# Attention of the second network: two heads at a time on halves of the array, and one VectorE pass for bias and maximum

## The chip, the cores and the metric

The kernel runs on one core of a Trainium2 chip. The metric is the device time of one execution in microseconds (us), as the median of several. The core has a matrix engine (TensorE, in the profile PE for the products and PEld for the loads of the stationary operand), VectorE (DVE), ScalarE (ACT), GpSimd (POOL) and SyncE (SP), which here issues most DMA transfers. The engines run side by side, each through its own list of instructions, and wait for one another by semaphores.

## The reference

Two networks are computed, one behind the other, each of attention mixers and feed-forward blocks on 256 context rows and 256 latent rows of width 1024. The change touches the two mixers of the second network. The first, called Mla here, has 8 heads with queries and keys of 128 "nope" and 64 "rope" columns; the rope part of the keys is shared by all heads. Latent rows see all 512 keys, context rows the 256 context keys:

```python
def _mla_kv(h, w_dkv, kv_norm, w_ukv, rows, cols):
    ckv = h @ w_dkv
    c_kv, k_pe = ckv[..., :MLA_KV_RANK], ckv[..., MLA_KV_RANK:]
    kv = (_rms_norm(c_kv, kv_norm) @ w_ukv).reshape(b, s, MLA_HEADS, MLA_NOPE + MLA_V)
    ...
def _mla_mixer(h, hc, w_dq, q_norm, w_uq, w_dkv, kv_norm, w_ukv, w_o, need_ctx):
    scale = (MLA_NOPE + MLA_ROPE) ** -0.5
    q = _mla_q(h, w_dq, q_norm, w_uq, rows, cols)
    k_all = jnp.concatenate([kc, k], 1)
    v_all = jnp.concatenate([vc, v], 1)
    out = _block_attention(q[:, :, :, None], k_all, v_all, scale) @ w_o
    if need_ctx:
        out_c = _block_attention(qc[:, :, :, None], kc, vc, scale) @ w_o
```

The second, called Na, has 16 heads of 64 columns. Latent rows see the 256 context keys and, with a bias and a mask, the 256 latent keys:

```python
s_lat = jnp.einsum('bqhd,bkhd->bhqk', q_row, k_strip).astype(jnp.float32) * scale + bias
s_lat = jnp.where(mask, s_lat, -jnp.inf)
s_ctx = jnp.einsum('bqhd,bkhd->bhqk', q_row, kc).astype(jnp.float32) * scale
p = jax.nn.softmax(jnp.concatenate([s_ctx, s_lat], -1), axis=-1).astype(v.dtype)
return jnp.einsum('bhqk,bkhd->bqhd', p, jnp.concatenate([vc, v_strip], 1))
```

## The kernel before

Activations are held transposed, with features on the 128 partitions. The projections around the attentions (L291 to L293) run three passes per tile, since each operand is split into a high and a low part; weights come by SyncE's DMA into `wraw`, and ScalarE (L221) and VectorE or GpSimd (L229) split them. Products land in eight PSUM banks that `bank()` hands out in turn, and `tt()` hands out the temporaries for exponentials and their transposes.

An attention is cut into units of one head and one block of 128 query rows. Mla has 32 units, 8 heads with row blocks `qt` in the order 2, 0, 3, 1, of which 2 and 3 have 512 keys and 0 and 1 have 256. Na has 32 units, 16 heads with two row blocks, all of 512 keys; two heads share a tile `t`, one on partitions 0 to 63 and one on 64 to 127 of queries and keys.

`attention()` walks through the units in steps and writes the order by hand: within `in_order`, TensorE, VectorE and ScalarE get their instructions in just the order in which the code issues them. In one step stand, for units of different age:

- the scores of the newest unit (`at_scores`, lag 0): Na L2318, on the 64 partitions of its head; Mla L2119 on all 128 partitions (nope) and L2123 on 64 (rope). Operands are fp32, and each such matmul is two passes.
- the turn of the unit of three steps ago (`at_turn`): transposes of the weights on TensorE L1972, 128 keys each, and a copy to `wT` on ScalarE L1974
- VectorE's part, woven instruction by instruction from three lists: the softmax of the newest unit (Na only: bias addition L2327, in PSUM on the 256 latent keys; then maximum L1953, its scaling L1954, with the exponential on ScalarE L1956), the normalization of the unit of two steps ago (reciprocal L1960, scaling L1961), and `lo`, the low part L1999 of a finished tile
- `hi`, the high part of a finished tile, copied by ScalarE L1992
- the value products of the unit of four steps ago (`at_out`): Mla L2147 on 128 columns, Na L2347 on the 64 columns of its head, which is `tile_position=(0, 64 * q)`. The tile of output is finished, and handed to `hi` of the next step, every four units in Na and in Mla.

Na's biases are chunks of 512 KB for two heads, in `wraw`; one is freed and one asked for every four steps. The last three steps (33 to 35) hold pieces of the output projection (`MLA_FILL`, `NA_FILL`), and Na's steps 28 to 31 split some of its weights on ScalarE and GpSimd. `low_apply` (rms norm and gain of Mla's queries and latent keys), `k_post` (Na's keys with their bias) and `prep` run ahead of the attentions.

Of the kernel before, what the change touches and what calls it, by code (L numbers as in the profile page):

```python
# [92 lines left out]
def build(nc, tc, ctx, A, stop=None):  # L93
# [1856 lines left out]
    def softmax(ps, nk, scale):  # L1950

        mx, rs = small(1), small(1)
        yield V.reduce_max(mx, ps[:, 0:nk], axis=AX.X)  # L1953
        yield V.tensor_scalar(mx, mx, -scale, None, ALU.mult)  # L1954
        e = tt()[:, 0:nk]
        ACT.activation(out=e, in_=ps[:, 0:nk], func=AF.Exp, scale=scale, bias=mx, accum_out=rs)  # L1956
        return e, rs
# [23 lines left out]
    def attention(units, mixer, before=lambda step: None, after=lambda step: None):  # L1981

        done, half = [], []

        def out(u):
            got = mixer.at_out(u)
            if got:
                done.append(got)
# [12 lines left out]
        def steps():  # L2001
            for step in range(len(units) + 4):
                before(step)
                at = {lag: units[step - lag] for lag in range(5) if 0 <= step - lag < len(units)}
                for lag, f in ((0, mixer.at_scores), (3, mixer.at_turn)):
                    if lag in at:
                        do(f, at[lag])
                do(lambda at=at: weave(*[f(at[lag]) for lag, f in ((0, mixer.at_soft), (2, mixer.at_norm)) if lag in at], lo()))
                do(hi)
                if 4 in at:  # L2010
                    do(out, at[4])
                after(step)
            do(hi)
            do(lambda: weave(lo()))
# [29 lines left out]
    class Mla:  # L2044
# [32 lines left out]
        def low_apply(self, name, nk, g):  # L2077
            M = self.M
            bc = rms_spread(M[name + "r"], FULL)
            M[name + "h"] = R[name] = h = HL(nk)  # L2080
            for k in range(nk):
                t = tt()[:, 0:512]
                V.scalar_tensor_tensor(t, M[name][:, k * 512:(k + 1) * 512], v(g, k), bc, ALU.mult, ALU.mult)
                split_act(t, h.at(0, k, FULL), h.at(1, k, FULL))
# [26 lines left out]
        def at_scores(self, u):  # L2111
            M = self.M
            hd, qt = u
            if "am" not in M:
                M["am"] = R["am"] = HL(8)
            nk = 256 if qt < 2 else 512
            ps = bank()
            o = hd % 4 * 512
            PE.matmul(ps[:, 0:nk], M["qn", hd // 4][:, o + qt * 128:o + qt * 128 + 128], M["kn", hd // 4][:, o:o + nk], start=True,  # L2119
                      stop=False)  # L2120
            p = slice(64 * (hd % 2), 64 * (hd % 2) + 64)
            o = hd // 2 * 512 + qt * 128
            PE.matmul(ps[:, 0:nk], M["qp", 0][p, o:o + 128], M["ckv"][p, 1024:1024 + nk], start=False, stop=True)  # L2123
            M["s", u] = ps

        def at_soft(self, u):
            M = self.M
            M["e", u] = yield from softmax(M.pop(("s", u)), 256 if u[1] < 2 else 512, (128 + 64) ** -0.5)
# [8 lines left out]
        def at_out(self, u):  # L2137
            M = self.M
            hd, qt = u
            nk = 256 if qt < 2 else 512  # L2140
            if qt == 2:
                M["po"] = bank()
            po = M["po"]
            wT = M.pop(("w", u))
            for j in range(nk // 128):
                vo = (j % 2) * 1024 + hd * 128
                PE.matmul(po[:, qt * 128:(qt + 1) * 128], M["v", j // 2][:, vo:vo + 128], wT[:, j * 128:(j + 1) * 128],  # L2147
                          start=j == 0, stop=j == nk // 128 - 1)
            if qt == 1:
                return po, hd, FULL  # L2150

        def middle(self):
# [42 lines left out]
            attention([(hd, qt) for hd in range(8) for qt in (2, 0, 3, 1)], self, early)  # L2195
# [63 lines left out]
    class Na:  # L2259
# [15 lines left out]
        def k_post(self, t, seg, ps):  # L2275
# [4 lines left out]
            ACT.activation(out=N["k", t // 4][:, o + seg.start:o + seg.stop], in_=ps, func=AF.Identity, bias=v("b_qk", 8 + t))  # L2280
# [29 lines left out]
        def at_scores(self, u):  # L2310
            N = self.N
            hd, qt = u
            if "am" not in N:
                N["am"] = R["am"] = HL(8)
            t, q = divmod(hd, 2)
            p = slice(64 * q, 64 * q + 64)
            ps = bank()
            PE.matmul(ps, N["q"][p, t * 256 + qt * 128:t * 256 + qt * 128 + 128], N["k", t // 4][p, (t % 4) * 512:(t % 4 + 1) * 512],  # L2318
                      start=True, stop=True)
            N["s", u] = ps  # L2320

        def at_soft(self, u):
# [4 lines left out]
            yield V.tensor_tensor(ps[:, 256:512], ps[:, 256:512], raw[:, bo:bo + 256], ALU.add)  # L2327
            N["e", u] = yield from softmax(ps, 512, 1.0)
# [8 lines left out]
        def at_out(self, u):  # L2337
            N = self.N
            hd, qt = u
            t, q = divmod(hd, 2)  # L2340
            if q == 0 and qt == 0:
                N["po"] = bank()
            po = N["po"]
            wT = N.pop(("w", u))
# [4 lines left out]
            if q == 1 and qt == 1:  # L2349
                return po[:, 0:256], t, X  # L2350

        def middle(self):
# [7 lines left out]
            units = [(hd, qt) for hd in range(16) for qt in range(2)]  # L2360
# [224 lines left out]
```

## Time and profile before

| | us |
|---|---|
| median of 3 runs (2868.4 to 2869.3) | 2868.72 |
| the profiled execution | 2867.64 |
| its span in the trace | 2865.9 |
| TensorE busy, products | 2780.0 (97%) |
| VectorE busy | 2012.6 (70%) |
| ScalarE busy | 1117.9 (39%) |
| GpSimd busy | 240.6 (8%) |

Busy time is counted over the whole span and says nothing of a single stage. The attention steps of Mla lie between 1902 and 1993 us after the span's start, those of Na between 2526 and 2621. A row of a timeline has the start in us, the duration, the engine, the line, the operation, what it writes and reads, the shapes of both (of a TensorE row first the rows and columns of the array that it uses), the number of instructions that stand in one row, and in brackets how long the engine idled before it, and for whom. A row of a table of windows has the stretch, its length, then each engine's busy time and number of instructions in the order PE, PEld, DVE, ACT, POOL, then the mean granted clock, the DMA share and GB/s. Recorded ends overlap the next start on the same engine a little, so the cost of a thing in a row of work is read from start to start.

### The profile page before, as it was taken

Reading aid. Unit: us, or ns where it says so; the run is one execution under the profiler, and the core shown is the slowest. Engines: PE = TensorE matmul, PEld = TensorE weight load, DVE = VectorE, ACT = ScalarE, POOL = GpSimd, SP = SyncE. Lnnn points to the kernel's source line nnn. Section 1 sums busy time; section 2 is a strip of 40 time slices with the busy share of each in tenths; the row PEclk is TensorE's granted clock in tenths of the full one; section 3 lists DMA queues with packets and bytes.
Section 4 is the critical chain, followed back from the end, with each engine's and each line's share of the span. In section 5 each row is a group of like instructions: output and inputs, shape, how many; then the busy total and the mean of one; then the engine's idle time right before and its main releaser. Section 6 shows DMA issues by size and latency. Waiting matters only on the chain. (4 is left out here: it accounts for less than half of the span.)

```text
span 2865.9 us, 41032 instructions
## 1 busy us (share of the span) xinstructions
PE 2780.0 (97%) x15940; PEld 2383.6 (83%) x15940; DVE 2012.6 (70%) x3847; ACT 1117.9 (39%) x1947; POOL 240.6 (8%) x184
## 2 busy tenths in 40 slices
PE   7999999999999999999999999999999999998998
PEld 4888888878888888888889999866888888966898
DVE  5877776567877788787845755734888848357766
ACT  3222235654222232222355544444522334335544
POOL 0000011221000010000210100100300003003200
PEclk9999999999999999999999999999999999999999
DMA  6655632112665636665532465320166631413453
GB/s 262 203 198 189 200 117 91 52 45 82 206 201 188 200 118 209 207 206 176 174 118 82 138 200 178 96 67 15 60 213 207 195 97 59 143 42 102 141 183 105
DMA packets 114068, 413.15 MB, mean 144 GB/s; under 512 B 12496, under 2 KB 14800, under 8 KB 112336
## 3 DMA queue, kind: packets, MB, share of 16 engines
q1 hardware_dynamic: 112256, 407.64, 44.0%
q10 hardware_dynamic: 1616, 2.88, 0.3%
q8 instruction: 125, 2.05, 0.3%
q14 instruction: 71, 0.58, 0.1%
HBM read 409.42 MB, written 1.05 MB: 143 GB/s over the span
## 5 line engine op out<-in xcount | busy, mean ns | idle before, releaser
L292 PE MATMUL p<-slot,whl 128*128 128x512 f32 (+2 forms) x4256 | 1444.3, 340 | 16.2 <-DVE slot L652 6.2
L291 PE MATMUL p<-slot,whl 128*128 128x512 f32 (+2 forms) x4256 | 1445.5, 342 | 6.3 <-ACT slot L589 2.9
L293 PE MATMUL p<-slot,whl 128*128 128x512 f32 (+2 forms) x4256 | 1440.6, 339 | 6.6 <-DVE whl L229 5.0
L292 PEld LDWEIGHTS p<-slot,whl 128*128 128x128 f32 x4256 | 811.1, 191 | 111.0 <-POOL slot L753 8.0
L291 PEld LDWEIGHTS p<-slot,whl 128*128 128x128 f32 x4256 | 807.7, 191 | 106.0 <-issue 8.2
L293 PEld LDWEIGHTS p<-slot,whl 128*128 128x128 f32 x4256 | 810.5, 191 | 94.9 <-DVE whl L229 6.5
L221 ACT ACTIVATE whl<-wraw 128x1024 fp32r<-128x1024 f32 (+1 forms) x527 | 542.8, 1043 | 510.5 <-PE p L293 292.0
L229 DVE TENSOR_TENSOR whl<-wraw,whl 128x1024 fp32r<-128x1024 f32 (+1 forms) x460 | 561.1, 1222 | 196.3 <-ACT whl L221 188.5
L396 DVE SCALAR_TENSOR_TENSOR t<-wraw,sB 128x1024 bf16<-128x1024 f32 x448 | 535.0, 1219 | 3.0 <-ACT sB L150 3.0
L229 POOL TENSOR_TENSOR whl<-wraw,whl 128x1024 fp32r<-128x1024 f32 (+1 forms) x67 | 166.8, 2497 | 2085.3 <-ACT whl L221 2059.8
L1069 ACT ACTIVATE t<-p 128x512 f32<-128x512 f32 (+1 forms) x86 | 47.2, 548 | 536.2 <-PE p L293 536.2
L1071 DVE TENSOR_TENSOR t<-t,p 128x512 f32<-128x512 f32 (+1 forms) x86 | 53.8, 626 | 215.0 <-PE p L293 158.0
L291 PE MATMUL p<-whl,slot 128*128 128x256 f32 (+1 forms) x432 | 126.2, 292 | 0.0
L292 PE MATMUL p<-whl,slot 128*128 128x256 f32 (+1 forms) x432 | 124.3, 288 | 1.8 <-DVE whl L229 1.8
L293 PE MATMUL p<-whl,slot 128*128 128x256 f32 (+1 forms) x432 | 124.0, 287 | 0.0
L811 DVE SCALAR_TENSOR_TENSOR xT<-p,mod,xT 128x256 f32<-128x256 f32 x192 | 86.0, 478 | 33.0 <-PE p L293 32.7
L590 DVE TENSOR_TENSOR slot<-t,slot 128x512 fp32r<-128x512 f32 (+1 forms) x166 | 101.5, 617 | 3.3 <-ACT slot L589 2.9
L589 ACT ACTIVATE slot<-t 128x512 fp32r<-128x512 f32 (+1 forms) x166 | 89.2, 541 | 19.1 <-DVE t L2228 7.6
L824 DVE SCALAR_TENSOR_TENSOR xT<-p,mod,xT 128x256 f32<-128x256 f32 x119 | 54.4, 479 | 50.5 <-PE p L293 50.1
L556 DVE TENSOR_TENSOR t<-t 128x256 f32<-128x256 f32 (+1 forms) x98 | 74.7, 762 | 19.6 <-ACT t L555 18.4
L291 PEld LDWEIGHTS p<-whl,slot 128*128 128x128 f32 x432 | 82.9, 192 | 4.0 <-issue 2.3
L292 PEld LDWEIGHTS p<-whl,slot 128*128 128x128 f32 x432 | 83.0, 192 | 3.4 <-DVE whl L229 2.2
(309 smaller groups left out, 2047.5 us busy)
## 6 DMA issues: line engine op xcount, KB each, us to landing
wraw<-in_ada SPq DMA_DIRECT2D x224, 512.0 KB, 4.1
wraw<-in_ffn_in SPq DMA_DIRECT2D x176, 512.0 KB, 4.4
wraw<-in_mlp SPq DMA_DIRECT2D x128, 512.0 KB, 3.6
wraw<-in_ffn_out SPq DMA_DIRECT2D x64, 512.0 KB, 4.4
wraw<-in_ffn_out SPq DMA_DIRECT2D x32, 384.0 KB, 3.8
slot<-in_ada SPq DMA_DIRECT2D x8, 1024.0 KB, 16.2
wraw<-in_even_a SPq DMA_DIRECT2D x16, 512.0 KB, 3.4
wraw<-in_odd_a SPq DMA_DIRECT2D x16, 512.0 KB, 3.6
```

What stands on the lines that cost most here:

```text
L221: ACT.activation(out=hl[:, 0, 0:n], in_=raw[:, 0:n], func=AF.Copy)
L229: eng.tensor_tensor(hl[:, 1, 0:n], raw[:, 0:n], f32(hl[:, 0, 0:n]), ALU.subtract)
L291: PE.matmul(ps, w[0], a[0], start=first, stop=False)
L292: PE.matmul(ps, w[0], a[1], start=False, stop=False)
L293: R["pe"] = PE.matmul(ps, w[1], a[0], start=False, stop=last).ins
L396: V.scalar_tensor_tensor(j.bitcast(BF16)[:, 0:1024], raw, 1.0, sB[:, r, :], ALU.mult, ALU.mult, accum_out=mods[li][:, f, r:r + 1])
L556: V.tensor_tensor(a, a, sq[:, seg], ALU.add)
L589: ACT.activation(out=hi, in_=src, func=AF.Copy)
L590: (eng or V).tensor_tensor(lo, src, f32(hi), ALU.subtract)
L811: V.scalar_tensor_tensor(xT[:, m, SEGS[s]], ps[:, q - seg.start:q - seg.start + 256], mod(li, gate)[:, m, s:s + 1], xT[:, m, SEGS[s]], ALU ...
L824: V.scalar_tensor_tensor(xT[:, m, SEGS[s]], ps[:, q - seg.start:q - seg.start + 256], mod(li, gate)[:, m, s:s + 1], xT[:, m, SEGS[s]], ALU ...
L1071: V.tensor_tensor(sa[:, 0:w], sa[:, 0:w], pb, ALU.mult)
```

## The change

Units are taken by two heads of the same row block. Scores are issued for two heads at once, on odd steps, for the two steps to come (the first two before step 0), and behind the turn. In Mla the nope products of both heads stand first, then the rope products, which use the two row halves; in Na the two heads' products use the two row halves. Value products are issued for two heads at once on odd steps; in Na they alternate between the two column halves.

Mla's score scale goes into the gain of the query norm, and its maximum is written negated, so that the scaling of the maximum falls away. Na's context keys are stored negated, and its exponential has scale −1; a minimum over the context keys (L2343 of the changed kernel) and one fused pass over the latent keys (L2344), which forms −(score + bias), writes it and takes the minimum along, take the place of bias addition, maximum and scaling.

```diff
-    def softmax(ps, nk, scale):
-        mx, rs = small(1), small(1)
-        yield V.reduce_max(mx, ps[:, 0:nk], axis=AX.X)
-        yield V.tensor_scalar(mx, mx, -scale, None, ALU.mult)
+    def exponentials(ps, nk, scale, mx):
+        rs = small(1)
         e = tt()[:, 0:nk]
         ACT.activation(out=e, in_=ps[:, 0:nk], func=AF.Exp, scale=scale, bias=mx, accum_out=rs)
...
         def steps():
+            do(mixer.at_scores, units[:2])
             for step in range(len(units) + 4):
...
-                for lag, f in ((0, mixer.at_scores), (3, mixer.at_turn)):
-                    if lag in at:
-                        do(f, at[lag])
+                if 3 in at:
+                    do(mixer.at_turn, at[3])
+                if step % 2 and step + 1 < len(units):
+                    do(mixer.at_scores, units[step + 1:step + 3])
...
-                if 4 in at:
-                    do(out, at[4])
+                if step % 2 and step >= 5:
+                    do(out, units[step - 5:step - 3])
...
         def low_apply(self, name, nk, g):
+            gain = v(g, 0, nk)
+            if name == "cq":
+                gain = small(nk)
+                V.tensor_scalar(gain, v(g, 0, nk), (128 + 64) ** -0.5, None, ALU.mult)
...
         def at_soft(self, u):
-            M["e", u] = yield from softmax(M.pop(("s", u)), 256 if u[1] < 2 else 512, (128 + 64) ** -0.5)
+            ps, nk, mx = M.pop(("s", u)), 256 if u[1] < 2 else 512, small(1)
+            yield V.reduce_max(mx, ps[:, 0:nk], axis=AX.X, negate=True)
+            M["e", u] = exponentials(ps, nk, 1.0, mx)
...
-            attention([(hd, qt) for hd in range(8) for qt in (2, 0, 3, 1)], self, early)
+            attention([(2 * p + q, qt) for p in range(4) for qt in (2, 0, 3, 1) for q in range(2)], self, early)
...
-            ACT.activation(out=N["k", t // 4][:, o + seg.start:o + seg.stop], in_=ps, func=AF.Identity, bias=v("b_qk", 8 + t))
+            if t == 0:
+                N["bk"] = small(8)
+                V.tensor_scalar(N["bk"], v("b_qk", 8, 8), -1.0, None, ALU.mult)
+            k = N["k", t // 4][:, o:o + 512]
+            ACT.activation(out=k[:, CTX], in_=ps[:, CTX], func=AF.Identity, scale=-1.0, bias=N["bk"][:, t:t + 1])
+            ACT.activation(out=k[:, X], in_=ps[:, X], func=AF.Identity, bias=v("b_qk", 8 + t))
...
-            yield V.tensor_tensor(ps[:, 256:512], ps[:, 256:512], raw[:, bo:bo + 256], ALU.add)
-            N["e", u] = yield from softmax(ps, 512, 1.0)
+            m, mx = small(1), small(1)
+            yield V.tensor_reduce(m, ps[:, 0:256], axis=AX.X, op=ALU.min)
+            yield V.tensor_tensor_reduce(ps[:, 256:512], ps[:, 256:512], raw[:, bo:bo + 256], -1.0, m, ALU.add, ALU.min, mx)
+            N["e", u] = exponentials(ps, 512, -1.0, mx)
...
             for j in range(4):
-                vo = (j % 2) * 1024 + hd * 64
-                PE.matmul(po[64 * q:64 * q + 64, qt * 128:(qt + 1) * 128], N["v", j // 2][:, vo:vo + 64],
-                          wT[:, j * 128:(j + 1) * 128], start=j == 0, stop=j == 3, tile_position=(0, 64 * q))
+                for q, wT in enumerate(wTs):
+                    vo = (j % 2) * 1024 + (2 * t + q) * 64
+                    PE.matmul(po[64 * q:64 * q + 64, qt * 128:(qt + 1) * 128], N["v", j // 2][:, vo:vo + 64],
+                              wT[:, j * 128:(j + 1) * 128], start=j == 0, stop=j == 3, tile_position=(0, 64 * q))
```

TensorE in Na's first steps, before (L2318 scores, L1972 transposes, L2347 value products):

```order
L2318 MATMUL p<-slot 128x512 x4
L1972 MATMUL p<-cst,t 128x128 x4
L2318 MATMUL p<-slot 128x512
L1972 MATMUL p<-cst,t 128x128 x4
L2347 MATMUL p<-t,slot 64x128 x4
L2318 MATMUL p<-slot 128x512
```

The same place of the changed kernel (L2334 scores, L1970 transposes, L2364 value products):

```order
L2334 MATMUL p<-slot 128x512 x4
L1970 MATMUL p<-cst,t 128x128 x4
L2334 MATMUL p<-slot 128x512 x2
L1970 MATMUL p<-cst,t 128x128 x8
L2334 MATMUL p<-slot 128x512 x2
L2364 MATMUL p<-t,slot 64x128 x8
L1970 MATMUL p<-cst,t 128x128 x8
```

Where one unit's transposes, value products and scores followed one another, now two units' scores, two units' value products (eight matmuls of two heads in alternation) and two units' transposes do.

VectorE near the end of Na, at a step with `lo` (L1999), before:

```order
L2327 TENSOR_TENSOR p<-p,wraw 128x256
L1960 RECIPROCAL tiny<-tiny 128x1
L1999 TENSOR_TENSOR slot<-p,slot 128x256
L1953 TENSOR_REDUCE tiny<-p 128x1
L1961 TENSOR_SCALAR t<-t,tiny 128x512
L1954 TENSOR_SCALAR tiny<-tiny 128x1
```

The same step of the changed kernel (L2343 minimum, L1958 reciprocal, L1996 `lo`, L2344 the fused pass and the read of its minimum, L1959 scaling by the reciprocal):

```order
L2343 TENSOR_REDUCE tiny<-p 128x1
L1958 RECIPROCAL tiny<-tiny 128x1
L1996 TENSOR_TENSOR slot<-p,slot 128x256
L2344 ISA p,tiny<-p,wraw,tiny 128x256
L2344 ISA tiny 128x1
L1959 TENSOR_SCALAR t<-t,tiny 128x512
```

`lo` stands behind the unit's first instruction and the reciprocal as before, now with the fused pass behind it; the scaling of the maximum, the unit's last instruction, is gone.

## Rows read from the trace of the kernel before

**Rows 1.** The page, busy time of each engine, its share of the span, instructions.

```profile
PE 2780.0 (97%) x15940; PEld 2383.6 (83%) x15940; DVE 2012.6 (70%) x3847; ACT 1117.9 (39%) x1947; POOL 240.6 (8%) x184
```

**Rows 2.** Windows: the attention steps of Mla, then those of Na.

```profile
1902.00:1992.80 90.80, 90.55 (x443) 54.22 (x442) 39.74 (x136) 41.86 (x106) 0.00 (x0) 1.00 0.03 9
2526.10:2621.30 95.20, 90.46 (x487) 55.51 (x485) 59.86 (x172) 49.46 (x111) 9.72 (x4) 0.96 0.22 67
```

**Rows 3.** Timeline of one unit in the middle of Na.

```profile
2546.48 0.42 PEld L1972 LDWEIGHTS p<-cst,t 128*128 128x128 f32 x4 [0.76 <-issue]
...
2546.59 0.43 DVE L2327 TENSOR_TENSOR p<-p,wraw 128x256 f32<-128x256 f32 x1 [1.04 <-PE p L2318]
...
2547.06 0.69 DVE L1953 TENSOR_REDUCE tiny<-p 128x1 f32<-128x512 f32 x1
2547.07 0.85 PEld L2347 LDWEIGHTS p<-t,slot 128*64 128x64 f32 x8 [0.17 <-issue]
...
2547.24 0.60 ACT L1974 ACTIVATE t<-p 128x512 f32<-128x512 f32 x1 [0.88 <-PE p L1972]
...
2548.06 0.15 DVE L1954 TENSOR_SCALAR tiny<-tiny 128x1 f32<-128x1 f32 x1
2548.09 0.29 PEld L2318 LDWEIGHTS p<-slot 64*128 64x128 f32 x2 [0.17 <-issue]
...
2548.24 0.69 ACT L1956 ACTIVATE t<-p,tiny 128x512 f32<-128x512 f32 x1 [0.40 <-DVE tiny L1954]
...
2548.92 0.38 ACT L1992 ACTIVATE slot<-p 128x256 fp32r<-128x256 f32 x1
2549.14 0.31 PEld L1972 LDWEIGHTS p<-cst,t 128*128 128x128 f32 x3 [0.76 <-issue]
...
2549.25 0.43 DVE L2327 TENSOR_TENSOR p<-p,wraw 128x256 f32<-128x256 f32 x1 [1.04 <-PE p L2318]
```

**Rows 4.** Timeline of two units of Mla, one of 256 and one of 512 keys.

```profile
1911.56 0.20 PEld L1972 LDWEIGHTS p<-cst,t 128*128 128x128 f32 x2 [0.76 <-ACT t L1956]
...
1912.62 0.30 PEld L2119 LDWEIGHTS p<-slot 128*128 128x128 f32 x2
...
1913.25 0.29 PEld L2123 LDWEIGHTS p<-slot 64*128 64x128 f32 x2 [0.33 <-issue]
...
1913.88 0.42 PEld L1972 LDWEIGHTS p<-cst,t 128*128 128x128 f32 x4 [0.33 <-issue]
...
1914.63 0.60 ACT L1974 ACTIVATE t<-p 128x512 f32<-128x512 f32 x1 [1.22 <-PE p L1972]
1914.71 0.30 PEld L2119 LDWEIGHTS p<-slot 128*128 128x128 f32 x2
...
1915.13 0.47 ACT L1956 ACTIVATE t<-p,tiny 128x256 f32<-128x256 f32 x1
...
1916.83 0.20 PEld L1972 LDWEIGHTS p<-cst,t 128*128 128x128 f32 x2 [0.76 <-issue]
```

**Rows 5.** Timeline: scores of Na's first four units, on alternating row halves.

```profile
2526.22 1.99 PE L2318 MATMUL p<-slot 64*128 64x512 f32 x8
```

**Rows 6.** Timeline: the first network's scores on two row halves, and what follows.

```profile
592.35 0.70 PE L1449 MATMUL p<-slot 64*128 64x256 f32 x4
...
592.98 0.19 PEld L291 LDWEIGHTS p<-whl,slot 128*128 128x128 f32 x1 [0.33 <-issue]
```

**Rows 7.** Timeline: products of the first network on column quarters (128 rows, 32 columns).

```profile
48.96 0.16 PEld L447 LDWEIGHTS p<-slot,t 128*32 128x32 f32 x8 [0.35 <-issue]
48.96 1.92 PE L447 MATMUL p<-slot,t 128*32 128x512 f32 x16
```

**Rows 8.** Line 396: count, minimum, median and maximum ns, first and last start.

```profile
L396 DVE SCALAR_TENSOR_TENSOR t<-wraw,sB x448: 1211/1219/1226, 67.1 to 2286.5; 128x1024 bf16<-128x1024 f32 x150
L396 DVE DVE_READ_ACCUMULATOR t<-wraw,sB x448: 76/84/88, 68.3 to 2287.6; 128x1 f32 x150
```

**Rows 9.** Groups of Na's stretch: `lo`; busy us, mean ns, idle before, releaser.

```profile
L1999 DVE TENSOR_TENSOR slot<-p,slot 128x256 fp32r<-128x256 f32 x8 | 3.3, 410 | 6.0 <-ACT slot L1992 6.0
```

More of the change, by code (lines that the diff above doesn't have):

```diff
@@ L1983, in attention, with out @@
         done, half = [], []
[L1985 to L1988, printed above, removed]
+        def out(us):
+            done.extend(mixer.at_out(us))
         def hi():
@@ L2082, in low_apply @@
                 t = tt()[:, 0:512]
-                V.scalar_tensor_tensor(t, M[name][:, k * 512:(k + 1) * 512], v(g, k), bc, ALU.mult, ALU.mult)
+                V.scalar_tensor_tensor(t, M[name][:, k * 512:(k + 1) * 512], gain[:, k:k + 1], bc, ALU.mult, ALU.mult)
                 split_act(t, h.at(0, k, FULL), h.at(1, k, FULL))
@@ L2135, in at_turn, with at_out @@
             M["w", u] = turn(M.pop(("e", u))[0], 256 if u[1] < 2 else 512)
-        def at_out(self, u):
+        def at_out(self, us):
             M = self.M
[L2139 to L2150, printed above, removed]
+            got = []
+            for hd, qt in us:
+                nk = 256 if qt < 2 else 512
+                if qt == 2:
+                    M["po", hd] = bank()
+                po = M["po", hd]
+                wT = M.pop(("w", (hd, qt)))
+                for j in range(nk // 128):
+                    vo = (j % 2) * 1024 + hd * 128
+                    PE.matmul(po[:, qt * 128:(qt + 1) * 128], M["v", j // 2][:, vo:vo + 128], wT[:, j * 128:(j + 1) * 128],
+                              start=j == 0, stop=j == nk // 128 - 1)
+                if qt == 1:
+                    got.append((M.pop(("po", hd)), hd, FULL))
+            return got
         def middle(self):
@@ L2308, in v_post, with at_scores @@
             return post
-        def at_scores(self, u):
+        def at_scores(self, us):
             N = self.N
-            hd, qt = u
             if "am" not in N:
                 N["am"] = R["am"] = HL(8)
[L2315 to L2320, printed above, removed]
+            for hd, qt in us:
+                t, q = divmod(hd, 2)
+                p = slice(64 * q, 64 * q + 64)
+                ps = N["s", (hd, qt)] = bank()
+                PE.matmul(ps, N["q"][p, t * 256 + qt * 128:t * 256 + qt * 128 + 128],
+                          N["k", t // 4][p, (t % 4) * 512:(t % 4 + 1) * 512], start=True, stop=True)
         def at_soft(self, u):
@@ L2359, in middle @@
                 body_B([("na_v", c, z) for z in range(2)], "h", FULL, self.v_post(c))
-            units = [(hd, qt) for hd in range(16) for qt in range(2)]
+            units = [(2 * t + q, qt) for t in range(8) for qt in range(2) for q in range(2)]
             self.out.begin()
```

37 lines of the change are left out of this document (19 added, 18 removed).

## The prediction

> **What bounds the kernel now.** First the engine shares of the page: TensorE is busy 97% of the span, VectorE 70%, ScalarE 39% [rows 1]. That is an average, so next the windows of the two stretches that the change rewrites, the steps of the Mla attention (1902.0 to 1992.8) and of the Na attention (2526.1 to 2621.3): TensorE is busy 90.55 of 90.80 us and 90.46 of 95.20, VectorE 39.74 and 59.86, ScalarE 41.86 and 49.46 [rows 2]. TensorE sets the pace of both, so only what shortens its own row of work can shorten them, and only as far as VectorE and ScalarE can follow. Of the 4.74 us that Na's stretch holds without TensorE, and of its clock of 0.96, I take nothing as changed.
>
> Now one Na unit, read from start to start of weight loads, since those show when TensorE turns to the next thing [rows 3]: transposes from 2546.48, value products from 2547.07, scores from 2548.09, the next transposes at 2549.14, so 0.59 + 1.02 + 1.05 = 2.66, and 32 × 2.66 = 85.1 us. VectorE in the same unit idles 1.04 for the scores and so works 2.66 − 1.04 = 1.62. Two Mla units (one of 512 keys, one of 256) take 1911.56 to 1916.83 = 5.27 us, the scores in them 1.26 (256 keys, 1912.62 to 1913.88) and 2.12 (512, 1914.71 to 1916.83) [rows 4]; 16 × 5.27 = 84.3 us.
>
> **The change part by part: TensorE.** Two things cost time in these products beside the columns. A 512-key Mla group of four passes takes 0.86 more than one of 256, so 256 columns more cost 0.215 a pass and 512 columns cost 0.43. Four passes would be 1.72; the group takes 2.12, so 0.40 goes into the turn from 128 rows to 64 and back. And a product on 64 rows or 64 columns leaves half of the array unused for its whole length.
>
> Row halves do run side by side where they follow one another: at the head of Na, four units on alternating halves, eight passes, take 1.99 [rows 5], where a single unit's two passes take 1.05 [rows 3]; and in the first network two heads on the two halves take 592.98 − 592.35 = 0.63 with 256 keys [rows 6], as much as one head's two rope passes in Mla (1913.25 to 1913.88 [rows 4]). So a pair's Na scores should take 1.05 in place of 2.10, and an Mla pair's four rope passes the time of two.
>
> Column halves are not in the trace; column quarters are: sixteen passes of 512 columns in 1.92, against 16 × 0.43 = 6.9 one after the other, and eight of their weight loads in 0.16 while the passes run [rows 7]. I take a pair's sixteen value passes as 1.02, the time of eight; the other end is 2.04. The Trainium skill ("TensorE: Matmul & The Clock Gate", Part 3: Packing small matmuls — row/col tiling, The mechanism) speaks against this edit: a weight load overlaps running matmuls "only when row_grp differs", and two column halves use the same rows. By that the value products would stay at 2.04 a pair; the column quarters, whose rows are the same as well, do not agree with it, yet they load only 32 columns at a time.
>
> The transposes lose one turn of the array per pair, since two groups no longer each stand between scores and values: 0.59 + 0.45 (four more at 0.11, since 1911.56 to 1912.62 holds ten such passes of 128 columns [rows 4]) = 1.04. **Na pair on TensorE:** 1.04 + 1.05 + 1.02 = 3.11, against 5.32.
>
> **Mla pair's scores on TensorE:** 512 keys 4 nope passes 1.72 + rope in the time of two 0.86 + one turn 0.40 = 2.98 against 4.24; 256 keys 0.86 + 0.43 + 0.40 = 1.69 against 2.52. Four units gain 1.26 + 0.83 = 2.09, 32 units 16.7.
>
> **VectorE and ScalarE as followers.** Na's softmax drops the 512-wide maximum (0.69) and the scaling of it (0.15); it gains a minimum over 256 keys, taken as long as the bias addition of the same width (0.43), and turns the bias addition (0.43) into a fused pass with an accumulator read [rows 3]. No such pass on 256 columns is in the trace. Lower bound: the plain addition, 0.43, and 0.08 for the read; upper: the nearest fused pass with a read, 1.22 on 1024 columns [rows 8], if it were to cost as much whatever the width. I take the lower, because 1.22 for four times the columns is 1.2 ns a column and 256 of them would be 0.31. VectorE's unit: 1.62 − 0.69 − 0.15 + 0.43 + 0.08 = 1.29, taken as 1.31. ScalarE's: copy 0.50 from its start to the next (1914.63 to 1915.13 [rows 4]), exponential 0.68 (2548.24 to 2548.92) and a quarter of the copy-out's 0.38 [rows 3]: 1.28. TensorE's half pair is 1.56. So TensorE still sets the pace, with only 0.25 to spare, and here the stall comes in.
>
> **The wait that takes some back.** Every fourth unit the finished tile is split: ScalarE copies it (hi, behind that step's copy and exponential), and VectorE's subtraction (lo, behind the next step's minimum and reciprocal) waits for it. It waits now too: 6.0 us over 8 times, 0.75 each [rows 9], hidden in VectorE's 1.04 of idle time per unit. After the change that cover is gone. Let a pair's scores start at S. VectorE begins the minimum at S + 1.16 (as the bias addition now, 2548.09 to 2549.25), and reaches lo one unit later, behind a second minimum and reciprocal (0.47, as from 2546.59 to 2547.06): S + 1.16 + 1.31 + 0.47 = S + 2.94. The next step's transposes start behind scores and values at S + 2.07, their copy 0.76 later (2546.48 to 2547.24) at S + 2.83, then 0.50, the exponential 0.68, hi 0.38: S + 4.39 [rows 3]. VectorE stands 1.45 with the fused pass and the scaling queued behind lo; ScalarE's next exponential waits for those, and TensorE's next transposes for it. That pair takes 2 × 1.31 + 1.45 + 0.32 (lo, 0.41 as recorded [rows 9], less the overlap with the next instruction) = 4.39 in place of 3.11. Four Na units: 3.11 + 4.39 = 7.50 against 10.64, a gain of 3.14. The last steps hold pieces of the projection and keep their length, and steps 28 to 31 have a weight split each on ScalarE, which may slow that group; I count 7.5 groups of eight: **Na −23.5**. In Mla the same place comes four times with two heads each; by Na's loss of 1.28 that is 5.1 (ends: 0, and twice that for the doubled tiles): **Mla −16.7 + 5.1 = −11.6**, taken as −11.
>
> **Small edits.** The keys leave ScalarE in two instructions of 256 (2 × 0.38) and not one of 512 (0.60): 8 × 0.16 = 1.3 if nothing hides them, nothing if the projection's products do; I count 0.6. The scaled gain of the query norm is one small VectorE instruction of 0.15, the negated bias another. The scale that Mla's softmax no longer needs takes 0.15 a unit off VectorE, which waits there anyway. SyncE's queue keeps its order; the bias chunks, one per four units, are now asked for every 7.5 us and not 10.6, on a DMA share of 0.22 [rows 2], which leaves room.
>
> **Sum.** 2867.64 (the profiled execution) − 23.5 − 11 + 0.6 = 2833.7; the median lies 1.1 above that execution, so 2834.8, **2835**.
>
> **The rivals.** *No stall* (0.10): the split work hides in the lag of three steps between softmax and transposes, and TensorE alone sets the pace: Na 15 pairs × 2.21 = 33.2, Mla 16.7, so 2868.7 − 49.9 + 0.6 = 2819. For it: the lag; against it: hi stands behind two instructions in an engine whose order is fixed.
>
> *Column halves in turn* (0.14): value products 2.04, pair 4.13 on TensorE. Then four Na units take 8.3 (two TensorE pairs) to 9.5 (with the stall, which grows by 1.02 as the transposes come later), a gain of 1.1 to 2.4: 2840 to 2850, middle 2845. This is what the quoted rule gives. For it: no halves in the trace; against it: the quarters.
>
> *Dear fused pass* (0.12): at 1.22, VectorE's unit becomes 1.29 − 0.51 + 1.30 = 2.08, above TensorE's 1.56. Four units 8.3 + a wait of 0.7 + 0.32 = 9.3, a gain of 1.3: −10 in Na, 2848.
>
> *Slower* (0.05): the same pass dearer still. With x for pass and read, a unit is 0.78 + x + 0.08 (a fourth of lo, which then waits for nothing) on VectorE; Mla's 11 are lost, and 5.7 more, once 32 units cost 16.7 more than now, at a unit of 3.18, x = 2.3. At twice the 1.22 and the read, 2.52, a unit is 3.38: 32 × 0.72 = 23.0, and 2868.7 + 23.0 − 11 + 0.6 = 2881.
>
> *The pairs don't meet* (0.04): halves run in turn throughout, because the second half's operands wait for a bank or a semaphore. Then a Na pair is 5.0 and Mla saves only the turns, 0.40 a pair, less the stall: 2868.7 − 5 − 1 = 2862, about no change.
>
> **How the numbers follow.** The forecast has 0.55. Its own bounds are a stall from none, 2819, to one twice as long, 7.5 × 1.45 = 10.9 more, 2846. With the second and third rival it holds 0.81, the first lies at the edge: the range is **2820 to 2850**. What a measurement can tell from no change is 0.2%, 5.7 us: faster means under 2863. The forecast and the first three rivals all are: 0.91. The last rival is split between same and faster. Faster 0.93, same 0.02, slower 0.05.
>
> **What would show it.** In the Na stretch of the changed kernel, starts of score loads two units apart: 3.1 and 4.4 in turn if I am right, 3.1 throughout for the first rival, 4.1 and more for the second with value loads 0.12 apart, the fused pass near 0.43 or near 1.2 for the third. VectorE's subtraction should wait about 1.4 for ScalarE, eight times. Mla's stretch should be near 80 us and Na's near 72. The forecast is wrong if TensorE is the longest row of neither.

## The result and the profile after

The changed kernel takes 2832.26 us (median of 4 runs, 2831.41 to 2833.45) against 2868.56 for the kernel before beside it: 0.9872 of its time, 95% interval 0.986 to 0.9885. The forecast was 2835, in a range of 2820 to 2850. Of the 36.3 us gained, 33.7 were forecast.

The page's row of engine busy time answers to [rows 1], the windows of Mla's and Na's attention steps to [rows 2]:

```profile
PE 2734.7 (97%) x15940; PEld 2363.8 (83%) x15940; DVE 2000.6 (71%) x3817; ACT 1112.1 (39%) x1955; POOL 240.8 (9%) x184
```

```profile
1903.90:1985.20 81.30, 76.42 (x445) 52.44 (x444) 36.67 (x103) 39.28 (x107) 0.00 (x0) 1.00 0.03 10
2519.00:2588.50 69.50, 58.77 (x492) 38.44 (x492) 50.84 (x173) 46.53 (x112) 9.93 (x4) 0.98 0.28 92
```

The share of TensorE on the whole page is still 97%, which shows why such a share says little. In the two stages it was 90.55 of 90.80 and 90.46 of 95.20; now it is 76.42 of 81.30 and 58.77 of 69.50. TensorE's work in Na fell by a third, and 10.7 us of the stage are now without it.

Two pairs of Na units, from the timeline of the changed kernel's trace. It answers to [rows 3]:

```profile
2530.28 0.30 PEld L2334 LDWEIGHTS p<-slot 64*128 64x128 f32 x4 [0.17 <-issue]
...
2531.33 0.85 PEld L2364 LDWEIGHTS p<-t,slot 128*64 128x64 f32 x16 [0.76 <-issue]
...
2531.44 0.43 DVE L2343 TENSOR_REDUCE tiny<-p 128x1 f32<-128x256 f32 x1 [0.61 <-PE p L2334]
...
2531.90 0.49 DVE L2344 CUSTOM_DVE_ANT_0 p<-p,wraw,tiny 128x256 f32<-128x256 f32 x1
...
2532.31 0.14 DVE L2344 DVE_READ_ACCUMULATOR2_ANT tiny<- 128x1 f32 x1
...
2532.36 0.97 PEld L1970 LDWEIGHTS p<-cst,t 128*128 128x128 f32 x8 [0.17 <-issue]
...
2532.70 0.42 DVE L2343 TENSOR_REDUCE tiny<-p 128x1 f32<-128x256 f32 x1
...
2533.49 0.30 PEld L2334 LDWEIGHTS p<-slot 64*128 64x128 f32 x4 [0.17 <-issue]
...
2533.61 0.68 ACT L1954 ACTIVATE t<-p,tiny 128x512 f32<-128x512 f32 x1
...
2534.27 0.38 ACT L1989 ACTIVATE slot<-p 128x256 fp32r<-128x256 f32 x1
...
2534.68 0.42 DVE L1996 TENSOR_TENSOR slot<-p,slot 128x256 fp32r<-128x256 f32 x1 [1.49 <-ACT slot L1989]
...
2535.66 0.69 ACT L1954 ACTIVATE t<-p,tiny 128x512 f32<-128x512 f32 x1 [0.52 <-DVE tiny L2344]
...
2536.02 0.42 PEld L1970 LDWEIGHTS p<-cst,t 128*128 128x128 f32 x4 [0.61 <-issue]
...
2537.28 0.42 PEld L1970 LDWEIGHTS p<-cst,t 128*128 128x128 f32 x4 [0.84 <-ACT t L1954]
...
2537.87 0.30 PEld L2334 LDWEIGHTS p<-slot 64*128 64x128 f32 x4 [0.17 <-issue]
```

From score load to score load the pairs take 3.21 (2530.28 to 2533.49) and 4.38 (to 2537.87), and so on in turn until the last scores. In the short pair three things follow without a gap that counts: scores 1.05, value products 1.03, transposes 1.13. In the long one VectorE's subtraction L1996 has waited 1.49 for ScalarE's copy L1989, which stood behind that step's exponential; the next exponential then waits 0.52 for VectorE, and the two groups of transposes come late.

Mla, score load to score load over four units, answers to [rows 4]:

```profile
1918.92 0.30 PEld L2126 LDWEIGHTS p<-slot 128*128 128x128 f32 x2
...
1921.89 0.97 PEld L2157 LDWEIGHTS p<-t,slot 128*128 128x128 f32 x8 [0.76 <-issue]
...
1923.44 0.73 PEld L2126 LDWEIGHTS p<-slot 128*128 128x128 f32 x4
...
1925.13 1.86 PEld L2157 LDWEIGHTS p<-t,slot 128*128 128x128 f32 x16 [0.33 <-issue]
...
1927.57 0.30 PEld L2126 LDWEIGHTS p<-slot 128*128 128x128 f32 x2
...
1934.52 0.69 DVE L1996 TENSOR_TENSOR slot<-p,slot 128x512 fp32r<-128x512 f32 x1 [2.04 <-ACT slot L1989]
```

The scores take 2.97 (512 keys) and 1.69 (256), four units 8.65 and no longer 10.54; where a pair of tiles is split, VectorE waits 2.04. From the first scores to the last subtraction L1996 (L1999 before) Mla takes 82.9 and no longer 92.3, Na 69.7 and no longer 95.9.

One thing in these spans is not the change's: Mla starts 1.9 us later than before (1903.86 against 1901.96) although all ahead of it but one small VectorE instruction is the same. In the runs below it starts anywhere from 1901.3 to 1907.2, later where the trace has TensorE at the lower clock for longer ahead of it: 20 us before, 27 in the changed kernel, 34 in the run that starts last. A profile is of one execution, some us above or below the median. So the experiments are read by the spacing of score loads inside a stage as well as by medians.

### The profile page after: what moved, and what is told of

Its sections match the earlier page's. It is cut to its first block, busy times and chain, and to the rows that moved or that the text cites. A ratio compares the mean times of both kernels' runs of the same rounds, so it can differ in the third digit from the quotient of the medians.

```text
span 2831.2 us, 41057 instructions
## 1 busy us (share of the span) xinstructions
PE 2734.7 (97%) x15940; PEld 2363.8 (83%) x15940; DVE 2000.6 (71%) x3817; ACT 1112.1 (39%) x1955; POOL 240.8 (9%) x184
## 3 DMA queue, kind: packets, MB, share of 16 engines
HBM read 409.42 MB, written 1.05 MB: 145 GB/s over the span
```

## The experiments

My theory: TensorE's row of work sets the pace of both stages; halves and pairs shorten it; VectorE's wait for ScalarE's copy gives part of it back. The rivals: column halves that don't meet, a dear fused pass, no stall. Two further parts had not been priced singly: issuing the scores ahead, and the clock.

### ScalarE's copy first

The copy of a finished tile goes to the head of the step; the subtraction stays where it was, one step behind it.

```diff
         def hi():
+            ready.extend(half)
+            half.clear()
             for po, k, seg in done:
...
-            while half:
-                po, k, seg = half.pop()
+            while ready:
+                po, k, seg = ready.pop()
...
                 before(step)
...
+                do(hi)
                 if 3 in at:
                     do(mixer.at_turn, at[3])
...
-                do(hi)
                 if step % 2 and step >= 5:
                     do(out, units[step - 5:step - 3])
...
             do(hi)
+            do(hi)
             do(lambda: weave(lo()))
```

> ScalarE's copy of a finished tile (hi) is issued at the head of the step, before the turn's copy and the exponential, and VectorE's subtraction (lo) stays one step behind it. Theory (the stall is the place of hi in ScalarE's order): in the changed kernel the value products end near 2532.4, yet hi runs only at 2534.27, and lo waits 1.49 for it. Put first, hi runs as soon as the products end, lo finds it done, and every pair of Na units takes 3.21 in place of 3.21 and 4.38 in turn: 7 x 1.17 = 8.2 in Na, 4 x 1.21 = 4.8 in Mla (9.86 against 8.65 per four units), 2832.3 - 13.0 = 2819. Rival (VectorE or ScalarE would be late in that pair anyway, and the wait only moves, since ScalarE now waits for the products ahead of the turn's copy): at most 3 us, 2829 or more.

It took 2826.07 us (2822.74 to 2829.24), 0.9848 of the kernel before (0.9833 to 0.9862). Its timeline at a tile's end:

```profile
2536.75 0.30 PEld L2337 LDWEIGHTS p<-slot 64*128 64x128 f32 x4 [0.17 <-issue]
...
2538.95 0.38 ACT L1991 ACTIVATE slot<-p 128x256 fp32r<-128x256 f32 x1 [0.15 <-PE p L2367]
...
2539.58 0.40 DVE L1998 TENSOR_TENSOR slot<-p,slot 128x256 fp32r<-128x256 f32 x1
...
2539.59 0.60 ACT L1972 ACTIVATE t<-p 128x512 f32<-128x512 f32 x1 [0.25 <-PE p L1970]
...
2539.96 0.30 PEld L2337 LDWEIGHTS p<-slot 64*128 64x128 f32 x4 [0.17 <-issue]
```

The copy waits 0.15 for the products, the subtraction for nothing, the turn's copy is not late, and this pair too takes 3.21. From the third pair on, all thirteen spacings of Na's score loads are 3.21 or 3.22. So the stall was the copy's place in ScalarE's order. The gain was below the 13 us expected since I counted stalls in places where there are none: the score starts of the changed kernel show two of 1.21 in Mla and five of 1.17 in Na (the others lie among the last steps, where projection pieces fill the time), 8.3 in all. A second run of it, beside the changed kernel, settles the size:

> The kernel with ScalarE's copy first again, beside the changed kernel in the same call, to tell a difference of some 8 us from executions that differ by 3 with the clock's falls. Theory (two stalls of 1.21 in Mla and five of 1.17 in Na go, by the score starts of the first run; 100.34 to 86.64 and 117.73 to 85.09 in the stages): 8.3 less than the changed kernel beside it, 2824. Rival (the stalls' time is given back behind the attentions): less than 3 us less.

> The changed kernel, for comparison in the same call: 2832.3, 36 us less than before.

2824.47 us (2823.77 to 2828.54) against 2833.88 (2832.6 to 2839.08), 0.9851 (0.9835 to 0.9868) and 0.9883 (0.9868 to 0.9898) of the kernel before: 9.4 us less, where 8.3 were expected. This version beats both kernels. (The stage lengths that the expectation quotes, 100.34 to 86.64 and 117.73 to 85.09, match no stretch that I find in the traces; the 8.3 comes from the spacing of the score starts.)

### Column halves in turn

```diff
-            for j in range(4):
-                for q, wT in enumerate(wTs):
+            for q, wT in enumerate(wTs):
+                for j in range(4):
```

> Na's value products of two heads are issued one head behind the other, so that the two column halves no longer alternate. Theory (the halves run side by side only where they alternate): a pair's value products take 2.04 from start to start in place of 1.02; four units take 8.3 (TensorE alone) to 9.5 (with the stall) in place of 7.60, 7.5 groups, 2837 to 2847. Rival (the halves overlap in any order, or the stall sets the pace whatever the products take): within 2 us of 2832.

2838.25 us (2836.58 to 2843.05). A pair's value products in its timeline, and what follows them:

```profile
2552.53 1.34 PEld L2364 LDWEIGHTS p<-t,slot 128*64 128x64 f32 x16 [0.76 <-issue]
...
2554.05 0.85 PEld L1970 LDWEIGHTS p<-cst,t 128*128 128x128 f32 x8 [0.17 <-DVE t L1959]
```

In turn the sixteen passes take 1.52, alternating 1.03 (2531.33 to 2532.36 above), and their weight loads 1.34 against 0.85. So column halves do run side by side, loads and products, and best where they alternate; the rule of the Trainium skill that the prediction weighed ("TensorE: Matmul & The Clock Gate", Part 3: Packing small matmuls — row/col tiling, The mechanism) does not hold for these. But in turn they cost 1.52 and not the 2.04 I had as the other end, and windows of these instructions alone show why (the first stretch of the pair's products, then the one behind it; the second count is of weight loads, and a load on an edge counts in both):

```profile
2552.53:2553.02 0.49, 0.48 (x4) 0.48 (x5) 1.00 0.84 92
2553.02:2553.40 0.38, 0.38 (x9) 0.38 (x8) 1.00 0.41 97
```

For 0.49 a load starts every 0.11, as with one head alone (eight in 0.85, [rows 3]); then they come twice as close, and behind 2553.40 at 0.11 again. So the second head's passes start beside the first head's last ones, 0.49 behind its first and not 1.02, and 0.49 + 1.03 is the 1.52. The theory's "only where they alternate" is wrong: in turn the halves overlap for about a third of the time. Four units take 8.08 (3.59 and 4.49 in turn), below the 8.3 expected: 0.49 more than with alternating halves, 2.8 over the middle of Na. About as much is lost in Na's head of the profiled execution (2843.05 us), where the clock fell (see the last experiment). That the median lies in the range expected doesn't bear out the sum of 8.3.

### The softmax of before, in pairs

```diff
-            ACT.activation(out=k[:, CTX], in_=ps[:, CTX], func=AF.Identity, scale=-1.0, bias=N["bk"][:, t:t + 1])
+            ACT.activation(out=k[:, CTX], in_=ps[:, CTX], func=AF.Identity, bias=v("b_qk", 8 + t))
...
-            m, mx = small(1), small(1)
-            yield V.tensor_reduce(m, ps[:, 0:256], axis=AX.X, op=ALU.min)
-            yield V.tensor_tensor_reduce(ps[:, 256:512], ps[:, 256:512], raw[:, bo:bo + 256], -1.0, m, ALU.add, ALU.min, mx)
-            N["e", u] = exponentials(ps, 512, -1.0, mx)
+            mx = small(1)
+            yield V.tensor_tensor(ps[:, 256:512], ps[:, 256:512], raw[:, bo:bo + 256], ALU.add)
+            yield V.reduce_max(mx, ps[:, 0:512], axis=AX.X)
+            yield V.tensor_scalar(mx, mx, -1.0, None, ALU.mult)
+            N["e", u] = exponentials(ps, 512, 1.0, mx)
```

> Na's softmax as before the change (bias addition, maximum over 512 keys, its scaling; context keys not negated), all else as changed. Theory (TensorE sets the pace with little to spare, and VectorE in the pair with the stall): VectorE's unit is 1.62 in place of 1.30, lo is reached 0.3 later and waits 1.1 to 1.2 in place of 1.49, so four units take 4 x 1.62 + 1.15 + 0.32 = 7.95, at most 3.24 + 5.0 = 8.25, in place of 7.60: 7.5 groups, 2835 to 2837. Rival (the fused pass carries the gain; without it VectorE is the bound throughout and the pairs are worth little): four units 9 or more, 2843 or more.

2839.4 us (2837.29 to 2842.76), 7 more than the changed kernel. Score loads and the subtraction between them:

```profile
2546.89 0.30 PEld L2334 LDWEIGHTS p<-slot 64*128 64x128 f32 x4 [0.17 <-issue]
2547.89 0.42 DVE L1996 TENSOR_TENSOR slot<-p,slot 128x256 fp32r<-128x256 f32 x1 [1.24 <-ACT slot L1989]
...
2551.53 0.30 PEld L2334 LDWEIGHTS p<-slot 64*128 64x128 f32 x4 [0.17 <-issue]
...
2554.95 0.30 PEld L2334 LDWEIGHTS p<-slot 64*128 64x128 f32 x4 [0.17 <-issue]
```

Four units take 4.64 + 3.42 = 8.06, a little above the 7.95 of the sum, and the wait is 1.24. So the fused pass is worth 0.46 per four units, 2.5 us from the fifth pair's scores to the last pair's, and 2.8 more are lost in Na's head, where three softmaxes stand ahead of the first turn: from the first scores to those of the fifth pair it takes 14.1 us (2521.33 to 2535.43) in place of 11.3, with the clock at 0.88 there; so a part of the 2.8 is the clock's (the profiled execution took 2842.76). Some 2 us of the medians' distance I can't place, and 2839.4 lies above the 2835 to 2837 expected. The fused pass is at most a fifth of the gain, not what carries it.

### Scores not ahead, and scores ahead alone

First the changed kernel, with a pair's scores issued in its own step:

```diff
-            do(mixer.at_scores, units[:2])
             for step in range(len(units) + 4):
...
-                if step % 2 and step + 1 < len(units):
-                    do(mixer.at_scores, units[step + 1:step + 3])
+                if step % 2 == 0 and step < len(units):
+                    do(mixer.at_scores, units[step:step + 2])
```

> Scores of two heads are issued on even steps for that step and the next, and not a step ahead. Theory (a pair's turn waits for the normalization that VectorE does behind this pair's first minimum): the second turn of a pair stands behind S + 1.16 + 1.3 and no longer behind S + 1.05, so TensorE waits about 1.4 in each pair; Na's pairs 4.5 in place of 3.8 on average, 16 x 0.7 = 11, and Mla's pairs lose some too, 0 to 10: 2843 to 2853. Rival (the lag of three steps between softmax and turn hides it): within 2 us of 2832.

2869.33 us (2865.2 to 2871.07), 0.9994 of the kernel before (0.9984 to 1.0003): the whole gain is gone. A pair of Na in its timeline:

```profile
2578.12 0.30 PEld L2333 LDWEIGHTS p<-slot 64*128 64x128 f32 x4 [0.17 <-issue]
...
2579.28 0.42 DVE L2342 TENSOR_REDUCE tiny<-p 128x1 f32<-128x256 f32 x1 [1.86 <-PE p L2333]
...
2580.15 0.48 DVE L1959 TENSOR_SCALAR t<-t,tiny 128x512 f32<-128x512 f32 x1
...
2580.75 0.42 PEld L1970 LDWEIGHTS p<-cst,t 128*128 128x128 f32 x4 [2.33 <-issue]
2580.78 0.63 PE L1970 MATMUL p<-cst,t 128*128 128x128 f32 x4 [1.53 <-DVE t L1959]
...
2582.95 0.30 PEld L2333 LDWEIGHTS p<-slot 64*128 64x128 f32 x4 [0.17 <-issue]
```

The theory's wait is there: TensorE stands 1.53 until VectorE has scaled a unit (L1959), which VectorE does behind the first minimum of the scores just issued. It was mis-sized, though: I put 1.4 on top of 3.11 for a pair of 4.5; measured are 4.83 (2578.12 to 2582.95) and 5.28 in turn, since scores to turn takes 2.63, and value products and two turns (2.20) all stand behind it. In Mla four units take 11.2, where 10.54 were before the change: TensorE waits 17.8 there between the first scores and the last, for the scaling (11.8) and for the exponential (6.0), and 0.2 before. From the first scores to the last subtraction Mla takes 97.2 (92.3 before) and Na 92.2 (95.9 before, with a fall of the clock in both heads), so the lost gain is a loss in Mla and a small gain in Na. One order was tried, with the scores behind the turn; with the scores ahead of it, as before, it may come out otherwise; no run shows that.

Then the reverse, the kernel before with nothing of the change but this:

```diff
+            do(mixer.at_scores, units[0])
             for step in range(len(units) + 4):
...
-                for lag, f in ((0, mixer.at_scores), (3, mixer.at_turn)):
-                    if lag in at:
-                        do(f, at[lag])
+                if 3 in at:
+                    do(mixer.at_turn, at[3])
+                if step + 1 < len(units):
+                    do(mixer.at_scores, units[step + 1])
```

> The kernel before with one thing of the change: scores of a unit are issued one step ahead, behind the turn; units singly, softmax and orders of products as before. Theory (TensorE's own row of work is the bound before the change, 90.55 of 90.80 us in Mla and 2.66 of 2.66 a Na unit, so nothing is waited for that earlier scores could free): 2868.6, within 3 us. Rival (scores issued ahead carry the gain by themselves, as the loss of all of it without them suggests): 2850 or less.

2871.18 us, 1.0013 of the kernel before (1.0002 to 1.0024): no gain. Score loads of two units one behind the other:

```profile
2569.60 0.29 PEld L2320 LDWEIGHTS p<-slot 64*128 64x128 f32 x2 [0.17 <-issue]
...
2572.26 0.29 PEld L2320 LDWEIGHTS p<-slot 64*128 64x128 f32 x2 [0.17 <-issue]
```

2.66 a unit, as in [rows 3]. So pairs without scores ahead (but with the fused pass) are worth nothing in all, scores ahead without pairs are worth nothing, and together they are worth 36 us. Before, TensorE's work covered the wait for the softmax; pairs take away the work, and with it the cover, unless the scores come earlier.

### Rope products in turn

```diff
                 PE.matmul(ps[:, 0:nk], M["qn", hd // 4][:, o + qt * 128:o + qt * 128 + 128], M["kn", hd // 4][:, o:o + nk],
                           start=True, stop=False)
-            for hd, qt, nk, ps in work:
                 p = slice(64 * (hd % 2), 64 * (hd % 2) + 64)
```

> In Mla's scores each head's nope products are followed by its own rope products, so the array turns twice a pair and the two row halves do not meet; all else as changed. Theory (the 0.40 of a turn and the overlap of the rope passes are the gain of the Mla part): a 512-key pair's scores take 2 x 2.12 = 4.24 in place of 2.97, a 256-key pair's 2.52 in place of 1.69, so four units take 8.65 + 2.10 = 10.75 and the 1.21 of the two pairs with a stall is partly covered: Mla's score starts spread over some 15 us more, 2846 to 2849. Rival (other waits, such as those for softmax and copy, take the place of the turn): less than half of that, under 2841.

2848.96 us (2846.93 to 2852.39), as the theory had it. Loads of TensorE over four units of Mla:

```profile
1918.32 0.30 PEld L2126 LDWEIGHTS p<-slot 128*128 128x128 f32 x2
1919.38 0.29 PEld L2130 LDWEIGHTS p<-slot 64*128 64x128 f32 x2 [0.76 <-issue]
...
1922.54 0.97 PEld L2156 LDWEIGHTS p<-t,slot 128*128 128x128 f32 x8 [0.76 <-issue]
...
1924.09 0.30 PEld L2126 LDWEIGHTS p<-slot 128*128 128x128 f32 x2
...
1929.04 0.30 PEld L2126 LDWEIGHTS p<-slot 128*128 128x128 f32 x2
```

The scores of a 512-key pair take 4.22 (1918.32 to 1922.54) and no longer 2.97, and four units 10.72 where 10.75 were expected. Of the 1.25, 0.86 is the time of two rope passes that no longer run beside the others (2 × 0.43) and 0.40 the second turn, both as estimated in the prediction. The score starts of the whole stage spread over 11.9 us more (77.14 against 65.27) and not 15, since four units with a stall cost only 0.4 more than four without, and the first eight units lose only 2.0 in all. The profiled execution took 2846.93, 14.0 more than the changed kernel's, which fits the 11.9 and a clock fall of 2.3 in Na's head (last experiment); the other 2.7 of the medians' distance I can't place.

### The weights' low parts on VectorE

The version with the copy first, with one more edit:

```diff
-                    items.extend([("hi",), ("lo", G)])
+                    items.extend([("hi",), ("lo", V)])
```

> As with ScalarE's copy first, and the four low parts of weights that Na's steps 28 to 31 form run on VectorE and not on GpSimd. In the run with the copy first, each of the four scalings L1959 beside GpSimd's 9.9 us takes 1.74 to 2.57 in place of 0.48, 8.9 in place of 1.9, and TensorE waits 2.0 for one of them. Theory (VectorE's scaling stands until GpSimd's instruction ends, so GpSimd's work costs VectorE more than doing it itself): 4 x 1.22 = 4.9 on VectorE in place of 7.0, scalings back at 0.48, and 1 to 3 us less than 2826. Rival (VectorE is the bound in those four units either way, 1.30 + 1.22 against TensorE's 1.61): 2826 or up to 3 us more.

2831.37 us (2829.13 to 2836.04), 0.9869 of the kernel before (0.9852 to 0.9885), against 2826.07 and 2824.47 without the edit. The intervals of the ratios overlap, but seven of the eight executions without it are shorter than all four with it: the edit gains nothing and most likely loses some 5 us, more than the rival allowed. The theory is half right. The groups of the last steps, first with the low parts on GpSimd (the copy-first version), then on VectorE (count, busy us, mean ns, idle before and releaser):

```profile
L229 POOL TENSOR_TENSOR whl<-wraw,whl 128x1024 fp32r<-128x1024 f32 x4 | 9.9, 2507 | 145.3 <-ACT whl L221 145.3
L1959 DVE TENSOR_SCALAR t<-t,tiny 128x512 f32<-128x512 f32 x5 | 9.4, 1880 | 0.0
```

```profile
L1970 PE MATMUL p<-cst,t 128*128 128x128 f32 x20 | 4.9, 395 | 6.5 <-DVE t L1959 6.5
L229 DVE TENSOR_TENSOR whl<-wraw,whl 128x1024 fp32r<-128x1024 f32 x4 | 4.9, 1226 | 7.0 <-ACT whl L221 7.0
L1959 DVE TENSOR_SCALAR t<-t,tiny 128x512 f32<-128x512 f32 x5 | 2.4, 483 | 0.0
```

The scalings are back at 0.48, so it was GpSimd's work that held them. But each low part now waits for ScalarE's high part with the next softmax queued behind it, 7.0 us over four, and TensorE waits 6.5. VectorE's time was not the price; its place in line was. How many us that costs by itself is open: in this profile (2836.04 us) the clock stands at 0.72 from the last scores on, and at 0.90 and 1.00 in the two profiles without the edit.

### The clock in Na's head

> The changed kernel once more, for one look at the clock in Na's head. Theory (the clock fall of 6.8 us in Na's head before is an event that the standstill there may or may not bring, and not something that the change removed): with the same standstill of 2.31 the granted clock falls to a half there in some executions (as in the run with the column halves in turn) and not in others (as in the changed kernel's first profile); a pair there then takes 4.4 or more in place of 3.22. Rival (the shorter standstill keeps the clock up, and the other run's longer products were the cause): no fall in the head here either.

One execution, 2832.57 us. Na's stretch from the first scores to those of the fifth pair, in the changed kernel's first profile, in this one, and in the run with rope products in turn, which does not touch Na (windows; the granted clock is the third number from the end):

```profile
2518.90:2530.30 11.40, 8.15 (x56) 4.26 (x54) 9.38 (x35) 6.59 (x16) 0.00 (x0) 1.00 0.16 47
```

```profile
2518.20:2529.60 11.40, 8.14 (x55) 4.28 (x54) 9.41 (x35) 6.62 (x16) 0.00 (x0) 1.00 0.14 47
```

```profile
2528.80:2542.50 13.70, 10.91 (x55) 5.65 (x54) 9.84 (x37) 6.50 (x16) 0.00 (x0) 0.75 0.12 39
```

The same instructions, and in all three TensorE stands 2.31 for the softmaxes of the first units before its first turn; then the clock falls to 1.2 GHz for a part of the stretch in one profile and stays at 2.4 in the others, 2.3 us of difference. This execution showed no fall, as the rival expected; but the rope run, and both profiles with products as in the changed kernel but a fall (low parts on VectorE; second run with the copy first), show that the longer products of the column run were not needed for one. So theory and rival are told apart by these, not by this run. Whether the change makes a fall rarer (the standstill before was 3.3) can't be told from so few profiles, and stays open.

## Why the prediction was right

**The pace.** TensorE's row of work was the right thing to count. Mla's scores came out as the sum had them: 2.97 and 1.69, where 2.98 and 1.69 were forecast. Na's pair takes 3.21 where 3.11 were; the transposes take 1.13, not 1.04.

**The stall.** Four Na units take 7.59 (7.50 forecast), and VectorE waits 1.49 (1.45), six times and not eight. Over the 22 units in the middle of Na the score starts spread over 41.20 us and no longer 58.46, a gain of 17.26; 5.5 groups of 3.14 are 17.27. The first rival, no stall, is out; the copy-first version is that rival made true, at 2824 where it was put at 2819.

One argument for it was misread, though. "It waits now too: 6.0 us over 8 times, 0.75 each" takes a group's total for its members: that row [rows 9] is one wait of 6.0 at Na's end, as the line's instructions in the trace of before show (here all 16, of both stages, with the waits and their number):

```profile
L1999 DVE TENSOR_TENSOR slot<-p,slot x16: 404/548/692, 1924.9 to 2621.7; 128x512 fp32r<-128x512 f32 x8, 128x256 fp32r<-128x256 f32 x8
...
  ACT slot L1992: 14.2, 3
```

Three waits, none in the middle of Na; the other two are in Mla's last steps. The forecast did not fall with it because the wait after was worked out from the order of instructions and their durations.

**The sizes.** Na gained more than the 23.5 forecast: 17.3 in the middle, 7.9 from the first scores to those of the ninth unit (2526.22 to 2545.43 before, 2518.96 to 2530.28 after), and 1.1 in the last steps up to the end of the value products, 26.3. Two steps were mis-sized: the last steps, which were to "keep their length", and "of its clock of 0.96, I take nothing as changed". In the profiled execution before, the clock fell in Na's head, in the one after it did not; with a fall, as in the rope run, the same head takes 2.3 longer, and the gain would have been 24.0. Mla gained 9.4 and not 11: 1.89 per four units and not 2.09, because the transposes cost more (1.32 per four units, 1.10 before), and 0.8 less than that in the first four; the two stalls of 1.21 that show between score starts, against four of 1.28 in the sum, gave some back. That Na's surplus and Mla's shortfall partly cancel, so that 2835 stands so near 2832.26, is luck, and the fall of the clock that this profile lacks is no merit of the sum.

**The fused pass** takes 0.49 and its read 0.14, where 0.43 and 0.08 were taken; VectorE's unit is 1.26 (2531.44 to 2532.70), taken as 1.31. The rival of the dear pass is out. **Column halves** meet, as forecast; the price of that rival was too high, 2.04 for 1.52, since in turn they still overlap in part. **Row halves** give a pair's Na scores in 1.05, as forecast, and not in 2.10; the traces show it, but no run turned this term off by itself.

**What the prediction left out** is the part that decides. It timed the scores one step ahead and never asked what the pairs would do without them. The step "the change part by part" should have had a term for it: scores in their own step make TensorE wait 1.53 in each pair of Na and 17.8 in all in Mla, and the pairs' whole gain is lost. The forecast was right with that part in place; it would not have told a reader which line of the change to keep.

## What to carry to other kernels

Shortening the engine that sets the pace takes away the cover under every wait that it hid: after the sum for its own row, walk the order of the other engines once with the new, shorter distances, and move what stands between a product and its follower (here a step ahead for the scores, and a copy to the head of a step). Price each part of a change without the others; here two parts were worth nothing singly and 36 us together. A group's idle total is one wait or many: look at the instructions before dividing by the count.

## What the runs showed of the hardware

- Grouping by the rows of the array pays twice: with the rope products behind each head's own nope products, a 512-key pair's scores take 4.22, with all nope products first 2.97. By the estimate from [rows 4], some 0.40 of that is one turn between 128 and 64 rows less, and 0.86 the rope passes on the two row halves running side by side.
- Column halves of the array load and run side by side: sixteen passes in 1.03 when two heads' instructions alternate, and 1.52 when they stand one head behind the other, since the second head then starts 0.49 behind the first.
- VectorE's scaling of 128x512 from SBUF to SBUF, 0.48 alone, took 1.7 to 2.6 beside GpSimd's four subtractions of 2.5 each, and 0.48 again without them; VectorE's passes on PSUM in the same stretch kept their time. The Trainium skill ("SBUF — State Buffer", Who interferes with whom) calls the port pair that the two share an exclusive lock, held for a whole instruction; the trace agrees for these scalings.
- The same standstill of 2.31 us was followed by a clock fall in three profiles (rope products in turn, low parts on VectorE, second run with the copy first) and not in four others, worth 1.3 to 2.3 us.
